# Chain outputs and the second norm's factors: turning on VectorE in 32 by 32 blocks, placed through DRAM

## The chip, the cores and the metric

The kernel runs on one core of a Trainium2 chip. The metric is the device time of one execution in microseconds (us). The profile comes from the hardware profiler and covers one execution. Its engines are PE (TensorE matmuls), PEld (TensorE weight loads, which overlap PE), DVE (VectorE), ACT (ScalarE), POOL (GpSimd) and SP (SyncE). SPq is the queue from which SP issues transfers. On each engine and on SPq, instructions run in the order in which the program placed them.

## What is computed

One layer of a hybrid decoder on 1024 tokens of width 1024, all in float32:

```
h = rmsnorm(x) * norm1_w ; proj = h @ w_in                 # columns split over two mixers
A: gated delta rule, 4 heads of 128, chunked, sequential in the chunks -> o_a
   o_a = rmsnorm(o_a, gdn_norm_w) * silu(z)
B: attention, 8 heads of 64, three dilated windows -> o_b
x = x + concat(o_a, o_b) @ w_out
h = rmsnorm(x, norm2_w)
u = causal_dwconv(h @ w_up) ; x = x + (silu(gate) * up) @ w_down
out = rmsnorm(x, final_norm_w)
```

`gdn_norm_w`, called the output weight here, has one value for each of the 128 columns of a head.

## The kernel before, in words

Most activations lie feature-major: 128 features on the partitions, 1024 tokens along the free dimension. Large products are split into a high and a low part and done in three passes (`mm3`, L200) on 128x512 blocks. Only the chain of the delta rule works with tokens on the partitions.

**Order of the work.** The kernel writes the order of TensorE's instructions by hand. `Weave` (L49) keeps a modelled clock. Work is written as generators ("streams"), each with a level, and the weave always takes the ready stream with the lowest level. A stream yields how long it wants to wait, from modelled ready times of its tiles (`wv.need`). Wrappers for the engines (L152 to L158) add the modelled duration of each instruction and transfer to those times. TensorE's instructions carry a token (`mm` L192, `tp` L196), so they keep the order in which the weave gave them. The instructions of the other engines and of SPq are ordered afterwards by a scheduler with its own timeline, which may move them before instructions that were written earlier. `uv` and `ua` are VectorE and ScalarE with a higher priority there.

**The streams that matter.**

- `dense()` (L532, level 9) runs the input projection column by column: 48 `mm3` passes each, with the next column's weights split one column ahead and the one after that loaded (`take`, L550). It fills whatever the other streams leave free on TensorE. Its last four columns are the gates z of the four chain heads. Column z of head h is taken only when `("o", h)` is done (L585). It then loads `og`, the head's normalised output, from DRAM and multiplies it with silu(z) (L608 to L611).
- `chain(h)` (L844, level 1), one for each head, walks 8 chunks. Each step goes over TensorE, VectorE (`r`, `wke`, the state `sn`) and ScalarE (`w`, `vtok`). At its end GpSimd scales the whole output `vtok` by the norm (L910) and `finish` is added.
- `finish(h, osb)` (L913, level 1) turns the output from token-major to feature-major. For each half of 512 tokens it transposes four 128x128 blocks on TensorE against the identity (`tp`), ScalarE copies the PSUM bank to `ot` with the output weight as its scale (`gw2`, half of `gdn_norm_w`), and one transfer writes 128 rows of 512 floats to `mixer` in DRAM. `ot` takes one of two slots (tag `t2`).
- `attention()` (L946, level 5) waits for `("o", h)` of all four heads and for two dense columns, then for each pair of heads runs scores, softmax, turning and values.
- `out_proj()` (L1144, level 8) takes the mixers' outputs, split in `mixer_splits` (L1119).
- `mlp_up()` (L1379, level 8) does the up projection in 22 channel tiles of 7 half-size products each (P1 to P7, `up`, L1316). `pa` is one PSUM bank in which P1, P6, P7 and P4 add up one after another; ScalarE copies its state after P1, P6 and P7 (`p1`, `u2`, `u3`).

**The second norm.** Each token's factor 1/rms must stand on all 128 partitions, because tokens lie along the free dimension (`rstdB`, 128x1024). In the first channel tile alone (`before is None`), `rms2_power` (L1236) sums the squares over the partitions on TensorE, VectorE adds the epsilon, and GpSimd takes the power -1/2; the result `rs` has 128 tokens on the partitions and 8 columns. P7 follows. Then `rms2_spread` (L1245) transposes each column, broadcast to 128 columns, on TensorE (8 transposes into two banks), and VectorE copies the banks to `rstdB`. P4 follows. VectorE first uses `rstdB` at L1357.

Of the kernel before, what the change touches and what calls it, by code (L numbers as in the profile page):

```python
# [147 lines left out]
def hybrid_layer(tc, I, out):  # L148
# [47 lines left out]
    def tp(dst, src, idt=None, us=0.11):  # L196
        tc.stamp_issue_order_token(nc.tensor.transpose(dst, src, ident if idt is None else idt).ins, TOKEN)  # L197
        wv.product(us, dst, src)
# [50 lines left out]
    def rsqrt(dst, src, n):  # L249
        po_.tensor_tensor(dst, src, mhalf[:, :n], op=OP.pow)  # L250
# [8 lines left out]
    vpark = dp.tile([S, 512], F32, name="vpark")  # L259
    qpark = dp.tile([H, P, S], F32, name="qpark")  # L260
    atpark = dp.tile([H, P, S], F32, name="atpark")
    xpark = dp.tile([KT, P, S], F32, name="xpark")
    upark = dp.tile([FT, P, S], F32, name="upark")

    def bank(tag, name="ps"):
        return tile_(pp_, (P, 512), F32, name, tag, 2)

    def next_bank(tag, *tiles, slack=0.0):

        while max(wv.need(*tiles), wv.slot_free(tag, 2)) + slack > 1e-3:  # L270
            yield max(wv.need(*tiles), wv.slot_free(tag, 2)) + slack
        return bank(tag)

    def half(i):
        return slice(i * 512, i * 512 + 512)
# [236 lines left out]
    def silu2(xr, name):  # L512
        y = A(name, "ev")
        ac.activation(y, xr, AF.Tanh, scale=0.5)
        ve.scalar_tensor_tensor(y, y, 1.0, xr, op0=OP.add, op1=OP.mult)
        return y
# [15 lines left out]
    def dense():  # L532

        yield from wv.until("first")
        yield from wv.until("norms")
        wv.add(2, first_keys())

        srcs, tiles = [], 0
        for col in DENSE:
            if col[0] == "V":  # L540
                srcs += [I["wv"][j] for j in range(4)]
            else:
                srcs.append(I["wi"][tiles])
                tiles += 1
        place = [0]
        raw = [raw_weight(srcs[0])]
        nxt = [weight(None, st=raw.pop())]
        raw.append(raw_weight(srcs[1]))

        def take():  # L550
            w = nxt.pop()
            i = place[0] = place[0] + 1
            if i < len(srcs):
                nxt.append(weight(None, st=raw.pop(), spare=i >= 17))
            if i + 1 < len(srcs):
                raw.append(raw_weight(srcs[i + 1]))
            return w

        def values_by_token(g):

            banks = [bank(t) for t in ("asc", "asc", "ch", "ch")]
            for j in range(4):
                w = [t.rearrange("p (k m) -> p k m", k=2) for t in take()]
                for kk in range(2):
                    k = 2 * j + kk
                    for i, pt in enumerate(banks):
                        c = 4 * g + i
                        yield wv.need(pt, *w)
                        mm3(pt, [t[:, c * P:(c + 1) * P] for t in xs[k]], [t[:, kk, :] for t in w], k == 0, k == KT - 1)
            for i in range(0, 4, 2):  # L570
                vx = A("vx", "ev", shape=(P, 2, 512))
                for e in range(2):
                    c = 4 * g + i + e
                    ac.activation(vx[:, e, :], banks[i + e], AF.Copy, scale=rst[:, c:c + 1])
                c = 4 * g + i
                sy.dma_start(vpark[c * P:(c + 2) * P].rearrange("(e p) d -> p e d", e=2), vx)
            wv.done.add(("V", g))

        for i, col in enumerate(DENSE):
            kind, h = col[:2]  # L580
            if kind == "V":
                yield from values_by_token(h)
                continue
            if kind == "z":
                yield from wv.until(("o", h))  # L585
            w = [t.rearrange("p (k m) -> p k m", k=KT) for t in take()]
            pair = []
            for hh in range(2):
                pt = bank("hf")
                yield wv.need(pt, *w)  # L590
                for k in range(KT):
                    mm3(pt, [t[:, k, :] for t in w], [t[:, half(hh)] for t in xs[k]], k == 0, k == KT - 1)
                    yield 0.0

                pair.append(pt)
                if hh == 0:
                    xr = A("aqkv" if kind == "a" else "xr", "go" if kind == "k" else "ev")
                scaled(pair, "xr", kind == "a", t=xr, hs=(hh,))
            if kind == "k":
                T["k", h] = conv_silu(xr, 4 + h, "kT", "kT*")  # L600
                wv.add(3, kprep(h))
            elif kind == "q":
                q = conv_silu(xr, h, "qT", "qa")
                wv.add(4, qprep(h, q))
            elif kind == "v":
                v = conv_silu(xr, 8 + h, "vT", "qa")
                wv.add(4, vprep(h, v))
            elif kind == "z":  # L608
                og = gated[h] = A("og", "kT*")
                sy.dma_start(og, mixer[h])  # L610
                ve.tensor_tensor(og, og, silu2(xr, "zz"), op=OP.mult)  # L611
            else:
                sy.dma_start(apark[h, col[2]], xr)
                wv.done.add(col)
        wv.done.add("dense")
# [295 lines left out]
        wv.add(1, finish(h, vtok))  # L911

    def finish(h, osb):  # L913
        for hh in range(2):
            pt = yield from next_bank("atr", osb)
            for c in range(4):
                i = 4 * hh + c
                tp(pt[:, c * P:(c + 1) * P], osb[:, i * P:(i + 1) * P])
            ot = tile_(sp, [P, 512], F32, "ot", "t2", 2)
            ac.activation(ot, pt, AF.Copy, scale=gw2)  # L920
            sy.dma_start(mixer[h][:, half(hh)], ot)
        wv.done.add(("o", h))


# [311 lines left out]
    def rms2_power():  # L1236
        ps = bank("atr")
        for c in range(NCH):
            mm(ps[:, c:c + 1], rstdB[:, c * P:(c + 1) * P], ones[:, :1], 0.215)
        rs = sp.tile([P, NCH], F32, name="rs")  # L1240
        uv.tensor_scalar(rs, ps[:, :NCH], 1.0 / 1024, EPS, op0=OP.mult, op1=OP.add)
        rsqrt(rs, rs, NCH)
        return rs

    def rms2_spread(rs):  # L1245
        for h in range(2):
            pb = bank("atr")
            for c in range(4):
                tp(pb[:, c * P:(c + 1) * P], rs[:, 4 * h + c:4 * h + c + 1].to_broadcast([P, P]))
            ve.tensor_copy(rstdB[:, half(h)], pb)  # L1250

    W = {}
    raws = {}
# [62 lines left out]
    def up(n, before):  # L1316

        xg, xu = A("xg", "kT"), A("xu", "kT")
        pa = bank("asc", "pa")
        yield from up_product(n, "P1", pa, True, False)  # L1320
        p1 = tile_(sp, [P, 512], F32, "p1", "t2", 2)
        ac.activation(p1, pa, AF.Copy)
        if before is not None:
            yield from before()
        pc = bank("ch", "pc")
        if before is None:

            yield from up_product(n, "P5", pc, True, False)
            pd = bank("hf", "pd")
            yield from up_product(n, "P2", pd, ks=range(3))  # L1330
        yield from up_product(n, "P6", pa, False, False)
        u2 = tile_(wp, [P, 512], F32, "u2", "wlo", 2)
        last["u2"] = ac.activation(u2, pa, AF.Copy)
        if before is None:
            yield from up_product(n, "P2", pd, False, ks=(3,))
            rs = rms2_power()
        else:
            yield from up_product(n, "P5", pc, True, False)
        yield from up_product(n, "P7", pa, False, False)
        if before is None:  # L1340
            rms2_spread(rs)
        else:
            pd = yield from next_bank("hf")
            yield from up_product(n, "P2", pd)
        u3 = tile_(sp, [P, 512], F32, "u3", "t2", 2)
        last["u3"] = ac.activation(u3, pa, AF.Copy)
        ve.tensor_tensor(xu[:, half(1)], u3, pc, op=OP.add)
        ve.tensor_tensor(xg[:, half(0)], p1, pd, op=OP.add)
        yield from up_product(n, "P4", pa, False, True)
        ac.activation(xu[:, half(0)], pa, AF.Copy)  # L1350

        def rest():
            yield from up_product(n, "P3", pc, False)
            ve.tensor_tensor(xg[:, half(1)], u2, pc, op=OP.add)
            del W[n]
            up_tail(n, xg, xu)
        ve.tensor_tensor(xu, xu, rstdB, op=OP.mult)  # L1357
        last["rest"] = rest
# [332 lines left out]
```

## Time and profile before

| what | before |
|---|---|
| time, median of 3 runs | 1200.84 us (1200.32 to 1201.92) |
| time of the profiled execution | 1200.36 us |
| its span | 1198.6 us |
| mean granted TensorE clock | 0.997 |
| DMA engines over the span | 154.80 MB, mean 129 GB/s |
| TensorE instructions, transposes of `finish` / of the second norm | 7050, of which 32 / 8 |
| chain of the delta rule | ends near 312 us |
| attention on TensorE | 319.5 to 442.8 us |
| second norm's factors | near 567 to 573 us |
| up projection, steady part | 577 to 976 us |

The profiled execution took 1200.36 us, 1.76 us more than its span from first to last instruction. In the views below, times are us from the start of the span unless marked ns. A row of a grouped view gives the line, the engine, the operation, its output and inputs by the program's names, how many there were, the busy time, the mean duration in ns of one, and the idle time of the engine just before them with what ended it. Where a helper issues the instruction, the line is the helper's: L142 and L144 are the engine wrappers, L193 is `mm` and L197 is `tp`. A matmul's row lasts longer than the matmul occupies TensorE, since they are pipelined: the distance from start to start is its cost.

### The profile page before, as it was taken

The numbers are of one execution on the slowest core, as the hardware profiler recorded it, in microseconds if no ns is written. First come the engines' busy times: TensorE is split into PE (matmuls) and PEld (weight loads), VectorE is DVE, ScalarE is ACT, GpSimd is POOL, SyncE is SP. The second block draws the span as 40 slices with busy tenths as digits, with TensorE's granted clock in tenths as the row PEclk, the third lists the DMA queues.
The fourth block names the chain that finished last, engine by engine and source line by source line (L and its number), as shares of the span: only waits on it lengthen the run. The fifth ranks groups of instructions, "written<-read, shape, count | busy, mean of one in ns | idle before, by whom it ended". The sixth has DMA issues, their size and how long they took to land.

```text
span 1198.6 us, 18324 instructions
## 1 busy us (share of the span) xinstructions
PE 1187.5 (99%) x7050; PEld 983.7 (82%) x7050; DVE 915.1 (76%) x1450; ACT 574.8 (48%) x1126; POOL 89.8 (7%) x100
## 2 busy tenths in 40 slices
PE   9999999999999999999999999999999999999997
PEld 7888888888777778888888888888888888888886
DVE  7683975665355566777989888989898889999875
ACT  7275345355454443655544544445445454434441
POOL 0212010214311120000000000000000000000000
PEclk9999999999999999999999999999999999999998
DMA  7435234436634204543213223131222398557414
GB/s 237 107 95 150 85 109 127 152 113 183 224 95 124 73 28 128 180 154 110 88 54 104 90 70 106 53 106 60 99 90 69 109 371 292 192 157 229 160 53 141
DMA packets 85798, 154.80 MB, mean 129 GB/s; under 512 B 21168, under 2 KB 36304, under 8 KB 85712
## 3 DMA queue, kind: packets, MB, share of 16 engines
q1 hardware_dynamic: 84848, 152.85, 39.1%
q8 instruction: 55, 0.90, 0.3%
q10 hardware_dynamic: 864, 0.79, 0.2%
q14 instruction: 31, 0.25, 0.1%
HBM read 117.68 MB, written 35.93 MB: 128 GB/s over the span
## 4 chain that ended last, share of the span: by engine, by line
PE 95%; DVE 2%; ACT 2%; issue 1%; DMA 0%; POOL 0%; POOLq 0%; DVEq 0%; SPq 0%; ACTq 0%
PE ps L193 45%; PE pa L193 20%; PE dw L193 17%; PE pc L193 10%; PE ps L197 3%; DVE kT L142 1%; ACT sm L144 0%; DMA xt<-in_xT 0%; DVE x1h L142 0%; ACT whi L142 0%; PE pd L193 0%; DVE zz L142 0%; ACT dec L142 0%; DVE xr L142 0%; DVE rstdB L142 0%
## 5 line engine op out<-in xcount | busy, mean ns | idle before, releaser
L193 PE MATMUL dw<-pr 128*128 128x512 f32 (+1 forms) x984 | 211.3, 376 | 0.0
L193 PEld LDWEIGHTS dw<-pr 128*128 128x128 f32 x984 | 176.7, 188 | 33.6
L193 PE MATMUL ps<-xhi,whi 128*128 128x512 f32 x384 | 157.7, 411 | 0.3 <-ACT xhi L144 0.3
L193 PE MATMUL ps<-xhi,wlo 128*128 128x512 f32 x384 | 150.3, 391 | 0.0
L193 PE MATMUL ps<-xlo,whi 128*128 128x512 f32 x384 | 148.4, 390 | 0.0
L193 PE MATMUL pa<-T,pair 128*128 128x512 f32 x528 | 127.0, 389 | 0.0
L193 PEld LDWEIGHTS pa<-T,pair 128*128 128x128 f32 x528 | 99.0, 188 | 20.6
L193 PEld LDWEIGHTS ps<-xhi,whi 128*128 128x128 f32 x384 | 72.5, 189 | 19.6 <-issue 5.6
L193 PEld LDWEIGHTS ps<-xhi,wlo 128*128 128x128 f32 x384 | 72.4, 188 | 15.7
L193 PEld LDWEIGHTS ps<-xlo,whi 128*128 128x128 f32 x384 | 72.3, 188 | 12.5
L142 ACT ACTIVATE u<-pa 128x512 f32<-128x512 f32 x44 | 26.3, 598 | 107.2 <-PE pa L193 107.2
L142 DVE SCALAR_TENSOR_TENSOR y<-xu,fcw,y 128x1023 f32<-128x1023 f32 (+1 forms) x44 | 56.4, 1281 | 22.1 <-ACT y L142 22.0
L142 ACT ACTIVATE whi<-wst 128x1024 fp32r<-128x1024 f32 x36 | 38.2, 1063 | 65.4 <-PE ps L193 54.3
L193 PE MATMUL pa<-B,A 128*128 128x512 f32 x264 | 63.4, 389 | 0.0
L193 PE MATMUL pa<-T,S 128*128 128x512 f32 x264 | 63.4, 389 | 0.0
L193 PE MATMUL pc<-B,pair 128*128 128x512 f32 x264 | 63.4, 389 | 0.0
L193 PE MATMUL pc<-T,S 128*128 128x512 f32 x264 | 63.4, 389 | 0.0
L142 DVE TENSOR_TENSOR wst<-wst 128x512 f32<-128x512 f32 x88 | 60.5, 688 | 0.9
L193 PE MATMUL ps<-B,pair 128*128 128x512 f32 x252 | 60.5, 389 | 0.0
L142 POOL TENSOR_TENSOR rs<-rs,mhalf 128x2 f32<-128x2 f32 (+2 forms) x4 | 4.7, 1187 | 738.4 <-DVE rs L144 738.4
L142 ACT ACTIVATE pr<-wd 128x1024 fp32r<-128x1024 f32 x33 | 34.9, 1058 | 49.5 <-PE dw L193 37.0
L144 ACT ACTIVATE sm<-sm,mx 128x128 f32<-128x128 f32 (+7 forms) x64 | 35.4, 556 | 48.2 <-DVE mx L144 48.2
(248 smaller groups left out, 2411.1 us busy)
## 6 DMA issues: line engine op xcount, KB each, us to landing
wst<-in_wu SPq DMA_DIRECT2D x44, 512.0 KB, 3.7
wd<-in_wd SPq DMA_DIRECT2D x44, 512.0 KB, 4.5
upark<-y SPq DMA_DIRECT2D x22, 512.0 KB, 3.6
wst<-in_wi SPq DMA_DIRECT2D x21, 512.0 KB, 3.8
r<-upark SPq DMA_DIRECT2D x11, 512.0 KB, 7.5
r<-upark SPq DMA_DIRECT2D x22, 256.0 KB, 7.5
wa<-in_wd SPq DMA_DIRECT2D x22, 256.0 KB, 3.3
wst<-in_wv SPq DMA_DIRECT2D x8, 512.0 KB, 3.7
```

The lines of the kernel that those rows point to most:

```text
L142: return getattr(eng, op)(*a, **kw)
L144: return getattr(eng, op)(*a, **kw)
L193: tc.stamp_issue_order_token(nc.tensor.matmul(dst, lhs, rhs, start=start, stop=stop, **kw).ins, TOKEN)
L197: tc.stamp_issue_order_token(nc.tensor.transpose(dst, src, ident if idt is None else idt).ins, TOKEN)
```

## The change

1. `finish` no longer uses TensorE or PSUM. VectorE turns each 128x512 half of `osb` in blocks of 32 by 32, which puts the elements of every block in place within it but leaves the blocks where they were. Four transfers per half, one for each group of 32 partitions, then write the pieces to a new DRAM tensor `odram`, in runs of 32 floats.
2. At the gate, four transfers (32 partitions each) in place of one load `og` from `odram`, in runs of 128 floats.
3. The output weight is no longer the scale of ScalarE's copy, which is gone. It joins the multiplication with the gate: one `scalar_tensor_tensor` in place of a `tensor_tensor`.
4. `rms2_spread` is gone. `rs` grows to 128x32, is filled with ones, its first 8 columns get the factors as before, and VectorE turns it by 32 by 32 blocks into `dt`. Four transfers write 8 rows of 32 floats each to `ndram` (1024 floats), and a fifth reads all 1024 floats to each of the 128 partitions of `rstdB`.

```diff
+    ndram = dp.tile([S], F32, name="ndram")
+    odram = dp.tile([H, 32, 4 * S], F32, name="odram")
...
                 og = gated[h] = A("og", "kT*")
-                sy.dma_start(og, mixer[h])
-                ve.tensor_tensor(og, og, silu2(xr, "zz"), op=OP.mult)
+                of = odram[h].rearrange("j (c a t) -> a j c t", c=NCH, a=4)
+                for a in range(4):
+                    sy.dma_start(v8(og)[32 * a:32 * a + 32], of[a])
+                ve.scalar_tensor_tensor(og, og, gw2, silu2(xr, "zz"), op0=OP.mult, op1=OP.mult)
...
     def finish(h, osb):
+        yield wv.need(osb)
         for hh in range(2):
-            pt = yield from next_bank("atr", osb)
-            for c in range(4):
-                i = 4 * hh + c
-                tp(pt[:, c * P:(c + 1) * P], osb[:, i * P:(i + 1) * P])
             ot = tile_(sp, [P, 512], F32, "ot", "t2", 2)
-            ac.activation(ot, pt, AF.Copy, scale=gw2)
-            sy.dma_start(mixer[h][:, half(hh)], ot)
+            ve.transpose(ot, osb[:, half(hh)])
+            to = odram[h].rearrange("j (f b i) -> b j f i", f=32, b=4)[:, :, 16 * hh:16 * hh + 16]
+            for b in range(4):
+                sy.dma_start(to[b], ot[32 * b:32 * b + 32].rearrange("p (f i) -> p f i", i=32))
...
-        rs = sp.tile([P, NCH], F32, name="rs")
-        uv.tensor_scalar(rs, ps[:, :NCH], 1.0 / 1024, EPS, op0=OP.mult, op1=OP.add)
-        rsqrt(rs, rs, NCH)
-        return rs
-
-    def rms2_spread(rs):
-        for h in range(2):
-            pb = bank("atr")
-            for c in range(4):
-                tp(pb[:, c * P:(c + 1) * P], rs[:, 4 * h + c:4 * h + c + 1].to_broadcast([P, P]))
-            ve.tensor_copy(rstdB[:, half(h)], pb)
+        rs = tile_(sp, [P, 32], F32, "rs", "dt", 2)
+        ve.memset(rs, 1.0)
+        uv.tensor_scalar(rs[:, :NCH], ps[:, :NCH], 1.0 / 1024, EPS, op0=OP.mult, op1=OP.add)
+        rsqrt(rs[:, :NCH], rs[:, :NCH], NCH)
+        dt = tile_(sp, [P, 32], F32, "dt", "dt", 2)
+        uv.transpose(dt, rs)
+        to = ndram.rearrange("(c t) -> c t", c=NCH)
+        for b in range(4):
+            sy.dma_start(to[:, 32 * b:32 * b + 32], dt[32 * b:32 * b + NCH, :])
+        sy.dma_start(rstdB, bass.AP(tensor=ndram.tensor, offset=ndram.offset, ap=[[0, P]] + list(ndram.ap)))
...
             yield from up_product(n, "P2", pd, False, ks=(3,))
-            rs = rms2_power()
+            rms2_power()
         else:
             yield from up_product(n, "P5", pc, True, False)
         yield from up_product(n, "P7", pa, False, False)
-        if before is None:
-            rms2_spread(rs)
-        else:
+        if before is not None:
             pd = yield from next_bank("hf")
             yield from up_product(n, "P2", pd)
```

## The prediction

> **What bounds the kernel now.** I read the page first: busy shares, then the chain that ended last.
>
> ```profile
> PE 1187.5 (99%) x7050; PEld 983.7 (82%) x7050; DVE 915.1 (76%) x1450; ACT 574.8 (48%) x1126; POOL 89.8 (7%) x100
> ...
> PE 95%; DVE 2%; ACT 2%; issue 1%; DMA 0%; POOL 0%; POOLq 0%; DVEq 0%; SPq 0%; ACTq 0%
> ```
>
> TensorE is 99% busy and is 95% of the chain: whatever leaves its queue leaves the end time, unless something it waits for becomes late. Busy shares overstate a pipelined engine, so the price of a transpose has to come from the chain in order of time, where each piece is what it adds to the path. These are the pieces on line L197 (`tp`) around the ends of the four chains, and the one of the second norm.
>
> ```profile
> 284.75 0.87 PE ps L197 x8
> ...
> 288.10 0.12 issue
> 288.23 0.63 PE ps L197 x4
> ...
> 290.00 0.44 PE ps L197 x4
> ...
> 299.13 0.44 PE ps L197 x4
> ...
> 300.48 0.44 PE ps L197 x4
> ...
> 311.21 0.87 PE ps L197 x8
> ...
> 570.05 0.87 PE ps L197 x8
> ```
>
> Columns: start, us on the chain, what. All 32 transposes of `finish` stand on the chain, about 0.11 us each, as do the 8 of the norm. Which stages can refill what goes? The table by stages answers that (length, then busy us and instruction count of PE, PEld, DVE, ACT, POOL, then the granted clock, DMA share and GB/s).
>
> ```profile
> 283.00:292.00 9.00, 8.88 (x63) 7.98 (x62) 4.44 (x13) 5.77 (x17) 4.41 (x5) 1.00 0.59 167
> 284.00:320.00 36.00, 35.88 (x203) 30.52 (x203) 11.30 (x26) 14.66 (x37) 15.64 (x10) 1.00 0.72 232
> 320.00:440.00 120.00, 119.61 (x1530) 92.81 (x1527) 70.96 (x243) 60.80 (x205) 23.55 (x45) 1.00 0.29 93
> 440.00:467.00 27.00, 27.00 (x158) 22.41 (x157) 14.70 (x14) 7.83 (x9) 2.40 (x1) 1.00 0.20 57
> ```
>
> From 284 to 320 dense columns fill TensorE between the chain's steps, and at 440 to 467 some 24 us of dense work are still left over after attention. So dense work can move up into every hole that a removed transpose leaves.
>
> **The change part by part.**
>
> *Transposes of `finish`, removed.* The six pieces: 0.87 + 0.63 + 3 x 0.44 + 0.87 = 3.69 us. The 0.12 us of issue ahead of the second may go too or stay; I leave it. **Gain 3.7 us**, bounds 3.3 (the eight sets counted from start to start, with the slower first product behind them kept) and 3.8.
>
> *Transposes of the norm, removed.* What comes next there decides.
>
> ```profile
> 567.08 2.97 PE L193 MATMUL pa<-T,pair 128*128 128x512 f32 x12
> ...
> 567.62 2.06 POOL L142 TENSOR_TENSOR rs<-rs,mhalf 128x8 f32<-128x8 f32 x1 [119.13 <-DVE rs L144]
> ...
> 569.89 1.03 PE L197 MATMUL ps<-ident,rs 128*128 128x128 f32 x8
> 570.15 0.60 ACT L142 ACTIVATE u<-pa 128x512 f32<-128x512 f32 x1 [1.29 <-PE pa L193]
> ...
> 570.80 3.01 PE L193 MATMUL pa<-T,pair 128*128 128x512 f32 x12
> ...
> 575.26 1.22 DVE L142 TENSOR_TENSOR xu<-xu,rstdB 128x1024 f32<-128x1024 f32 x1
> ...
> 579.09 2.88 PE L193 MATMUL pa<-T,S 128*128 128x512 f32 x12
> ```
>
> P7 (567.08) and P4 (570.80) add into the same bank `pa`, and ScalarE must copy its state between them (`u3`, 570.15 to 570.75, released by P7's last product). In later channel tiles P2 covers that copy; in this one P2 was done earlier, and the 8 transposes are the only cover. Take them out and P4 still starts at about 570.80, behind the copy. The 0.87 us turns into idle time. **Gain 0.05 us**, the distance from the copy's end to P4's start; bounds 0 and 0.1.
>
> *VectorE's transposes, added.* The trace has none. Nearest rows:
>
> ```profile
> L142 DVE TENSOR_TENSOR wst<-wst 128x512 f32<-128x512 f32 x88 | 60.5, 688 | 0.9
> ...
> L142 DVE TENSOR_TENSOR aqkv<-ps,rstdB 128x512 f32<-128x512 f32 x16 | 17.8, 1112 | 21.7 <-PE ps L193 21.7
> ```
>
> A plain pass over 128x512 takes 0.69 us, one with scattered columns 1.11. I take 0.69 (both sides are read and written once) and keep 0 and 1.11. Eight make 5.5 us, bounds 0 and 8.9, against 24.7 us in which VectorE is idle between 284 and 320: room in sum. ScalarE loses its eight copies. What is queued behind a transpose on VectorE are the steps `r`, `wke` and the state of the heads still running, and TensorE waits for those in a fixed order. That matters for heads 0 and 1 (283 to 292), where VectorE is busy 4.44 of 9 us; heads 2 and 3 end in quiet stretches. **Loss 0.5 us**: four transposes there, each with an even chance to stand ahead of a due step, half of one (0.34) in the mean, gives 0.7, of which dense products cover a part; bounds 0 and 4 x 0.69 = 2.8. The Trainium skill (VectorE: DVE Perf Modes, The three transpose paths) gives 311 ns for a 128x128 bf16 turn on VectorE and advises TensorE for 128x128. By an estimate from that page a half would take 1.24 us and the loss would be 0.9. No run so far shows it.
>
> *Transfers, added.* SPq issues 32 writes and 16 loads in place of 8 and 4, and 5 for the norm.
>
> ```profile
> L142 SPq DMA_DIRECT2D x<-xdram x8: 319/484/487, 173.6 to 181.1; - x8
> ...
> q1 hardware_dynamic: 8203, 1.01, 48.8%
> ...
> q1 hardware_dynamic: 975, 0.15, 52.7%
> ...
> L142 DVE TENSOR_TENSOR og<-og,zz x4: 1224/1225/1226, 424.4 to 470.3; 128x1024 f32<-128x1024 f32 x4
> ...
> 301.30 0.39 SPq L142 DMA_DIRECT2D wst<-in_wi  x1
> ...
> wst<-in_wi SPq DMA_DIRECT2D x2, 512.0 KB, 4.5
> ...
> 322.27 1.04 ACT L142 ACTIVATE whi<-wst 128x1024 fp32r<-128x1024 f32 x1
> ```
>
> The first row is a transfer of 512 pieces of 128 bytes, as each new write is: 0.484 us to issue. So 36 more issues cost SPq some 17 us over 40 us. The two queue rows price a piece: in 173 to 186 us (reads of 128 bytes) 0.488 x 13 x 16 / 8203 = 12.4 ns; in 111.5 to 113.7 us (writes of 128 bytes) 0.527 x 2.2 x 16 / 975 = 19 ns. The new writes are 32 x 512 pieces: 16384 x 19 / 16 = 19.5 us of all engines. The old writes, 2.1 MB at 232 / 0.72 = 322 GB/s, took 6.5. The stretch of 36 us, 25.8 us full, then needs about 39: the queue falls some 3 us behind, and the loads of `og` in short rows may double that. What is late then? `og` is loaded soon after 290 and used at 424.4 at the earliest, as its row shows. The tightest transfer behind it is a weight tile: issued at 301.30, landing 4.5 us later, split at 322.27, so 16 us spare. **Cost 0**, and 1 us for each us beyond 16 if that cover goes.
>
> *Gate.* Four `scalar_tensor_tensor` stand for four `tensor_tensor` of the same size, one pass each, beside dense products from 424 us on. **0**, bounds 0 and the 0.4 us by which the scattered pass above exceeds the plain one, if the last head's gate were to end a wait.
>
> *The factors through DRAM.* The power ends at 569.68, the turn of 128x32 about 0.2 later; SPq is free there.
>
> ```profile
> wst<-in_wu SPq DMA_DIRECT2D x44, 512.0 KB, 3.7
> ...
> dec<-gdram SPq DMA_DIRECT2D x4, 512.0 KB, 7.6
> ...
> gdram<-grow SPq DMA_DIRECT2D x1, 16.0 KB, 1.4
> ...
> 577.73 0.33 SPq L142 DMA_DIRECT2D wst<-in_wu  x1
> ```
>
> Four issues (1.6), a small write landing (1.4 to 2.0) and a 512 KB read: 3.7 as a weight tile, 7.6 as the other broadcast, which had three more beside it. I take 3.7: `rstdB` at about 577.3, bounds 576.5 and 581.5, against 575.26 where VectorE used it. VectorE is held about 2 us (bounds 0 and 6); behind it stand the weight splits of the next channel tile, and on SPq the weight load of 577.73. The first product needing one of the held splits comes 5 us or more later (the next `pa<-T,S` at 579.09 has its operand by 573.6), so it stays hidden; **cost 0**, bounds 0 and 1.
>
> *Order.* The weave models every added transfer at 0.78 us on SPq (per-half writes) and 1.5 (loads), so attention, which starts 8 us after the last `finish`, is placed about 4 us later, with dense columns in front of it. TensorE idles 0.39 us in attention's 120, so a new order can't win there; **0** taken, loss up to the third rival's price.
>
> **Sum** against the profiled span: 1198.6 - 3.7 - 0.05 + 0.5 = 1195.35; with the 1.76 us around it 1197.1. The median of the runs, 1200.84, lies 0.48 above the profiled execution's 1200.36, so against the median I say **1197.5**.
>
> **The rivals.**
>
> *Half of the gain more* (1195.5): the slower first products and the issue gaps go as well, and the handover costs nothing. Price: the gain at its upper bound of 3.8 with the loss of 0.5 gone is 1196.6, and a dense product behind each of eight sets, slowed today by the switch, may give another 1.1. For: the pieces of 0.44 and 0.87 hold only the transposes. Against: chain steps of the same kind stand next to most sets and keep that cost.
>
> *No change: `ot`'s two slots hold VectorE* (1200.4).
>
> ```profile
> mixer<-ot SPq DMA_DIRECT2D x8, 256.0 KB, 4.4
> ...
> 285.43 1.90 POOL L142 TENSOR_TENSOR vtok<-vtok,ms 128x1024 f32<-128x1024 f32 x1
> ...
> 289.02 0.69 ACT L142 ACTIVATE ot<-ps,gw 128x512 f32<-128x512 f32 x1 [0.23 <-DMA mixer<-ot]
> ...
> 291.84 0.35 DVE L144 TENSOR_SCALAR wke<-ps,ke 128x128 f32<-128x128 f32 x1 [2.37 <-PE ps L193]
> ```
>
> Head 1 ends 4 us after head 0 and needs the same two slots, each free only when four small transfers have landed. Head 0's first half, issued from 284.5, lands near 289, its second near 291.5; head 1's output is ready at 287.3. If both turns sit in VectorE's queue at that time, it is held 1.7 + 1.8 = 3.5 us with chain steps behind, which eats the 3.7. For: the old transfers took 4.4 us to land here, and 0.23 us of such a wait stands in the trace of ScalarE. Against: VectorE idles 2.37 us at 289.5 anyway, and the scheduler puts a turn where it believes the slot free.
>
> *Slower: attention in its new order waits for the softmax* (1204.6).
>
> ```profile
> PEld ps L197 <- ACT sm L144: 2.5, 12, 0.4
> ```
>
> Today 12 of attention's 32 turns wait for ScalarE's exponentials, 2.5 us in all, 0.4 the longest. The order is made so that dense products lie in between; shifted by 4 us and with columns pulled ahead, the gaps fall elsewhere. If all 32 wait 0.4 us, that is 12.8, or 10.3 more: 1207; with the mean of 0.21 it is 6.7, or 4.2 more: 1201.4; I price it between at 7.4 more. It decides from 6.1 us (3.7 and the 2.4 that count as slower). For: the weave's slacks suit one order. Against: 24 us of dense work remain to fill with.
>
> *Slower: short writes are dear* (1216). If a written piece of 128 bytes costs over 30 ns, the stretch to 320 needs 25.8 - 6.5 + 1024 x 0.030 = 50 us, 14 behind, and the weight tile comes late; at four times the read piece, 50 ns, it is 34 behind and TensorE waits some 19 us. Against: the measured 19 ns. The Trainium skill (DMA: Bandwidth & Descriptors, Specifications) says that transfers under 512 bytes are done as read-modify-write, which is this case; the 19 against 12.4 ns agree in direction only.
>
> **How the numbers follow.** 0.2% is 2.4 us, about what a measurement of this kernel tells from no change: faster means below 1198.4, slower above 1203.2. Chances: forecast 0.46, the larger gain 0.06, `ot`'s slots 0.23, softmax 0.18, short writes 0.07. Hence faster 0.52, same 0.23, slower 0.25. The forecast's own range is 1196.3 to 1198.4. To hold 8 in 10, the range takes the larger gain's lower side at 1195.0 and the middle of the softmax rival at 1204.5; the rest of that one and the short writes, under 2 in 10, stay out.
>
> **What would show it.** Right: no L197 piece between 284 and 312; P4 of the first channel tile still behind ScalarE's copy with a hole of 0.8 us on TensorE; the multiplication by `rstdB` released by a transfer 1 to 3 us later than now, and TensorE gapless behind it; `og` landed tens of us before use. Wrong: VectorE's transposes with an idle time ended by `odram` transfers and chain products waiting; attention's turns with more than 2.5 us behind ScalarE; a weight split waiting for its transfer; or TensorE idle over 1 us between 575 and 600.

## The result, and the profile after

| | before | after |
|---|---|---|
| time, median of 4 runs | 1200.64 us (1200.32 to 1201.92, taken beside those of after) | 1215.85 us (1214.26 to 1217.01) |
| ratio to before | 1 | 1.0127, 95% interval [1.0114, 1.014] |
| span of the profiled execution | 1198.6 us | 1212.5 us |
| mean granted TensorE clock | 0.997 | 0.992 |

The kernel became 15 us slower. The forecast was 1197.5, and the range ended at 1204.5. The busy shares on the page of after:

```profile
PE 1190.8 (98%) x7010; PEld 983.7 (81%) x7010; DVE 914.8 (75%) x1458; ACT 569.3 (47%) x1118; POOL 90.1 (7%) x100
```

TensorE has 40 instructions fewer and is busy 3.3 us longer, and its idle time in the span grew from 11.1 to 21.7 us. So something both holds it and slows it down. The table by stages of after says where (columns as in the prediction):

```profile
284.00:320.00 36.00, 34.34 (x175) 28.63 (x173) 16.16 (x34) 9.63 (x30) 15.18 (x11) 1.00 0.85 196
...
440.00:460.00 20.00, 14.63 (x208) 11.28 (x209) 17.60 (x45) 15.12 (x42) 1.87 (x7) 0.92 0.47 147
460.00:470.00 10.00, 8.13 (x98) 5.49 (x96) 5.89 (x18) 5.68 (x18) 0.59 (x2) 0.67 0.15 51
470.00:484.00 14.00, 13.06 (x139) 9.41 (x136) 5.65 (x18) 5.08 (x16) 0.59 (x2) 0.86 0.12 39
```

Between 440 and 484 TensorE idles 5.37 + 1.87 + 0.94 = 8.2 us, and the granted clock falls to 0.92, 0.67 and 0.86. A low clock costs only while TensorE works, so its price is taken from steps of 2 us: busy time times the missing share of the clock is 6.0 us (the rows and the sum stand in the last section). Together that is 14.2 us. In the kernel before, the same stretch was full at clock 1.00. What TensorE waited for there stands in the waits of after between 320 and 490 (waiter, releaser, us in total, times, longest) and in its timeline:

```profile
PEld ps L197 <- ACT sm L144: 11.6, 22, 3.0
...
PE ps L197 <- ACT sm L144: 7.4, 12, 2.8
```

```profile
455.56 0.92 PE L197 MATMUL ps<-ident,sm 64*128 64x64 f32 x12 [2.77 <-ACT sm L144]
457.62 0.58 PE L197 MATMUL ps<-ident,sm 64*128 64x64 f32 x6 [1.14 <-ACT sm L144]
```

Attention's turns wait for the exponentials, as in the prediction's third rival, but here TensorE has nothing at all to do in between. The reason is older than 440. The starts of attention's groups of scores on TensorE, first in before and then in after:

```profile
319.54 0.93 PE L193 MATMUL ps<-kT,qT 64*128 64x128 f32 x8
324.07 1.47 PE L193 MATMUL ps<-kT,qT 64*128 64x256 f32 x40
330.33 1.68 PE L193 MATMUL ps<-kT,qT 64*128 64x256 f32 x40
```

```profile
325.53 0.93 PE L193 MATMUL ps<-kT,qT 64*128 64x128 f32 x8
336.88 1.47 PE L193 MATMUL ps<-kT,qT 64*128 64x256 f32 x40
364.91 1.68 PE L193 MATMUL ps<-kT,qT 64*128 64x256 f32 x40
```

The third group comes 34.6 us later than before, and in the gap TensorE is full: it does dense columns. The gate of the last dense columns shows how far these ran ahead: it ran from 424.4 to 470.3 before, and runs from 375.0 to 452.6 now.

```profile
L142 DVE SCALAR_TENSOR_TENSOR og<-og,gw,zz x4: 1252/1254/1268, 375.0 to 452.6; 128x1024 f32<-128x1024 f32 x4
```

The dense work that used to lie between attention's steps until 467 is used up early, and the last part of attention stands alone.

### The profile page after: what moved, and what is told of

The parts are those of the page before. It is cut to its first block, busy times and chain, and to the rows that moved or that the text cites. A ratio compares the mean times of both kernels' runs of the same rounds, so it can differ in the third digit from the quotient of the medians.

```text
span 1212.5 us, 18290 instructions
## 1 busy us (share of the span) xinstructions
PE 1190.8 (98%) x7010; PEld 983.7 (81%) x7010; DVE 914.8 (75%) x1458; ACT 569.3 (47%) x1118; POOL 90.1 (7%) x100
## 4 chain that ended last, share of the span: by engine, by line
PE 91%; ACT 3%; DVE 3%; issue 1%; DMA 1%; SPq 0%; POOLq 0%; POOL 0%; DVEq 0%; ACTq 0%
PE ps L193 43%; PE pa L193 20%; PE dw L193 17%; PE pc L193 10%; PE ps L197 2%; ACT sm L144 1%; DVE kT L142 1%; DMA ot<-mixer 1%; DMA xt<-in_xT 0%; ACT whi L142 0%; DVE x1h L142 0%; ACT zz L142 0%; PE pd L193 0%; DVE og L142 0%; DVE oT L142 0%
## 5 line engine op out<-in xcount | busy, mean ns | idle before, releaser
L142 ACT ACTIVATE pr<-r 128x1024 fp32r<-128x1024 f32 (+1 forms) x44 | 36.5, 839 | 49.2 <-PE dw L193 29.0
```

What stands on the lines that cost most here:

```text
L142: return getattr(eng, op)(*a, **kw)
```

## The experiments

**Theory.** The order is made by the weave's clock, and the clock is wrong about the new writes. `account`, the function that enters an instruction or a transfer into that clock, lets an entry begin only when every tensor that it names is ready. All writes name `odram`, so each is charged behind the landing of the one ahead: 0.78 + 2.2 = 2.98 us apiece. The turn of head 3's second half needs the `ot` slot that was filled two halves earlier, and so the 24th write, 24 x 2.98 = 71.5 us after the first. Until then the clock keeps that head's `vtok`, whose slot (tag `dv*`) attention's softmax takes next. Counted from the first write's issue at 283.5 that is 355, on a clock that runs some us apart from the trace; the trace has the third group at 364.91. This way through `ot` and `vtok` is read from the program; no run isolates it. On the chip, the writes do not wait for each other: head 0's eight were issued in 4.14 us, where the clock charges 8 x 2.98 = 23.8, and a write landed in 2.0 us (median). These are after's rows of the queue and of the transfers:

```profile
283.46 4.14 SPq L142 DMA_DIRECT2D odram<-ot  x8
```

```profile
odram<-ot SPq DMA_DIRECT2D x32, 64.0 KB, 2.0
```

**Rivals:** the short transfers are themselves slow (the prediction's last rival, which named 1216), or VectorE's turns and `ot`'s slots hold the chain.

The times of this section are medians of up to 11 runs, each with its ratio to before on the same chip. Before was 1200.21 beside e1 to e4, 1200.26 beside e5 to e8 and 1199.84 beside e9 to e12. The ratio can differ from that of the two medians by up to 0.06%, or 0.7 us.

### e1_model: after, with the clock charged as in before

```diff
-                    sy.dma_start(v8(og)[32 * a:32 * a + 32], of[a])
+                    nc.sync.dma_start(v8(og)[32 * a:32 * a + 32], of[a])
+                wv.account("sync", 0.05 + 0.00142 * 1024, [og], [odram], 2.2)
...
-                sy.dma_start(to[b], ot[32 * b:32 * b + 32].rearrange("p (f i) -> p f i", i=32))
+                nc.sync.dma_start(to[b], ot[32 * b:32 * b + 32].rearrange("p (f i) -> p f i", i=32))
+            wv.account("sync", 0.05 + 0.00142 * 512, [odram], [ot], 2.2)
```

> The changed kernel with every instruction and transfer kept; only the weave's clock is charged as before: one transfer of 0.78 us per half and one of 1.50 us for og, in place of four each, which the clock puts one behind the other because all four write the same tensor. Theory A (the loss is an order of products made for transfers that the clock took to be long: attention's third group of scores placed 28 us late, dense columns used up ahead of it): attention's groups come every 7 us from the first on, dense products last past attention, 1197.5 us, between 1196 and 1199.5. Theory B (the loss is on the chip: short writes and a held queue): 1211 or more, as the same transfers run. Theory C (both, VectorE held by ot's two slots near 287 us): 1199.5 to 1202.

Measured: **1198.63 us, ratio 0.9991 [0.9982, 1.0000]**. The same instructions and the same transfers as after, 17.2 us less (16.3 by the two ratios). Its rows for the stretch of above, and its third group of scores:

```profile
440.00:460.00 20.00, 20.00 (x89) 16.55 (x89) 11.25 (x10) 5.08 (x6) 2.40 (x1) 1.00 0.18 52
460.00:470.00 10.00, 9.88 (x43) 7.52 (x42) 8.18 (x8) 4.98 (x6) 0.00 (x0) 1.00 0.58 174
470.00:484.00 14.00, 14.00 (x64) 11.58 (x63) 6.03 (x9) 4.84 (x8) 0.00 (x0) 1.00 0.35 122
```

```profile
331.22 1.68 PE L193 MATMUL ps<-kT,qT 64*128 64x256 f32 x40
```

The hole and the low clock are gone; the third group of scores starts at 331.22. The profiled span is 1196.6 us, 15.9 less than that of after, and the 14.2 us found above are most of it; the other 1.7 us are not assigned. This refutes the short writes as the cause: the number that rival gave was right by accident.

### e2_clock: before, with the clock charged as in after

```diff
+                for _ in range(3):
+                    wv.account("sync", 0.05 + 0.00142 * 1024, [og], [mixer], 2.2)
                 sy.dma_start(og, mixer[h])
...
+            wv.account("vector", 0.0, [ot], [osb], 0.28)
             sy.dma_start(mixer[h][:, half(hh)], ot)
+            for _ in range(3):
+                wv.account("sync", 0.05 + 0.00142 * 512, [mixer], [ot], 2.2)
```

> The kernel before, with no instruction or transfer added; only its clock is charged with the entries of the changed kernel (three more transfers per half in finish, three more for og, and a turn on VectorE that needs ot's slot). Theory A: the order alone costs it, attention ends after the dense products and stands without cover: 1212 to 1220 us. Theory B: nothing on the chip changed, 1200.6, at most 2 us more.

Measured: **1221.58 us, ratio 1.0184 [1.0169, 1.0200]**. No instruction of the change is in it, and it loses 21.4 us, more than after did; its time lies 1.6 us above the expected range. Its clock is not that of after in every entry: the tensor that its entries share is `mixer`, to which attention's outputs go as well. Its tail has the same picture, first the wait, then a row of its table by stages:

```profile
PEld ps L197 <- ACT sm L144: 15.4, 22, 7.1
```

```profile
460.00:480.00 20.00, 9.66 (x134) 6.53 (x118) 12.13 (x30) 9.55 (x24) 0.59 (x2) 0.64 0.38 125
```

### e9_single: after, with every transfer charged by itself

This is what the prediction took the clock to do. `Own` is a name that no other entry shares.

```diff
+                    wv.account("sync", 0.05 + 0.00142 * 1024, [og if a == 3 else Own(("og", h, a))], [Own((h, 1, 3))], 2.2)
...
+                wv.account("sync", 0.05 + 0.00142 * 512, [Own((h, hh, b))], [ot], 2.2)
```

> This is the whole change with every one of its transfers charged in the modelled clock by itself (0.78 us of SPq for each write, 1.5 for each load, no transfer waiting for another one's tensor), which is what the prediction assumed of the clock. If the slow order comes from the writes being charged one behind another through the one DRAM tensor, the clock now releases the chain's tiles 1.5 to 3.5 us after each finish instead of 20 to 45, attention gets back the order of before, and the time is that of e1_model: 1198.6 (1198.0 to 1199.3). If the mere number of charged transfers on SPq is what spoils the order, the time stays above 1203 and attention's turns wait for the exponentials 5 us or more.

Measured: **1199.08 us, ratio 0.9996 [0.9987, 1.0004]**. Attention begins late, at 325.70, as in after, but the third group follows at 336.64, and the turns' wait is small (the class `Own` moves the lines of this kernel by six, so L199 is `mm`, L203 is `tp` and L150 the wrapper):

```profile
336.64 1.68 PE L199 MATMUL ps<-kT,qT 64*128 64x256 f32 x40
```

```profile
PEld ps L203 <- ACT sm L150: 1.8, 9, 0.4
```

So the number of charged transfers does no harm that the time shows, and a late start of attention does none either. What does it is that they are charged one behind another. This run frees the loads of `og` as well as the writes, so the share of each is not told apart.

### e3_norm: before, with the norm part alone

```diff
-            rs = rms2_power()
+            rms2_power()
...
-        if before is None:
-            rms2_spread(rs)
-        else:
+        if before is not None:
```

(with `rms2_power` as in the change)

> The kernel before with the second norm's part of the change alone (turn of 128x32 on VectorE, four small writes, one broadcast read). By the prediction's step: P4 still starts behind ScalarE's copy, so 0.05 us gained and nothing lost, 1200.6 us, between 1199.9 and 1201.2, with a hole of 0.8 us on TensorE ahead of P4. Rival: VectorE held some 3 us by the read delays weight splits and TensorE waits, 1202 or more.

Measured: **1200.34 us, ratio 1.0002 [0.9993, 1.0011]**. The norm part is worth nothing that the time shows. After's rows for TensorE (the product that sums the squares, P7, P4) say why:

```profile
579.26 1.84 PE L193 MATMUL ps<-ones,rstdB 128*128 128x1 f32 x16
580.96 2.97 PE L193 MATMUL pa<-T,pair 128*128 128x512 f32 x12
584.68 3.01 PE L193 MATMUL pa<-T,pair 128*128 128x512 f32 x12 [0.75 <-ACT u L142]
```

P4 waits for ScalarE's copy. From the start of the sum of squares to P7's it is 1.70 us here and was 1.70 before; to P4's it is 5.42 and was 5.42. Eight transposes went, and a hole of about their length came.

### e4_chain: the chain part alone, with the clock of e1_model

The norm is that of before; the rest is e1_model.

> The clock charged as in e1_model, the chain's part of the change kept, the second norm as before. Theory A with the norm's part worth nothing: as e1_model within 0.5 us, 1197.5. If the norm's part costs anything on the chip, this one is faster than e1_model by that much (1 us or more if VectorE's wait for the read reaches TensorE).

Measured: **1198.54 us, ratio 0.9988 [0.9979, 0.9997]**. The chain part nets 1.7 us (1.4 by the ratio) where its 32 transposes were priced at 3.7. The next runs ask where the other 2 us are. In the stretch from 284 to 320 TensorE idles 1.56 us, where before idled 0.12. After has the same two holes, shown by its TensorE rows and by VectorE's. `r,um` is the product whose result `wke` scales:

```profile
282.87 0.38 PE L193 MATMUL ps<-r,um 128*128 128x128 f32 x2
285.77 0.49 PE L193 MATMUL ps<-wke,ktok 128*128 128x128 f32 x2 [0.91 <-ACT w L144]
290.23 0.49 PE L193 MATMUL ps<-ct,kT 128*128 128x128 f32 x2 [0.75 <-DVE ct L144]
```

```profile
282.72 0.71 DVE L142 STREAM_TRANSPOSE ot<-vtok 128x512 f32<-128x512 f32 x1
283.58 0.70 DVE L142 STREAM_TRANSPOSE ot<-vtok 128x512 f32<-128x512 f32 x1
284.20 1.03 DVE L142 TENSOR_TENSOR aqkv<-ps,rstdB 128x512 f32<-128x512 f32 x1
285.10 0.32 DVE L144 TENSOR_SCALAR wke<-ps,ke 128x128 f32<-128x128 f32 x1
287.02 0.71 DVE L142 STREAM_TRANSPOSE ot<-vtok 128x512 f32<-128x512 f32 x1 [0.37 <-DMA odram<-ot]
289.24 0.71 DVE L142 STREAM_TRANSPOSE ot<-vtok 128x512 f32<-128x512 f32 x1 [0.76 <-DMA odram<-ot]
```

Head 0's turns and a dense `aqkv` stand ahead of `wke`, and ScalarE's `w` follows `wke`: 0.91 us. Head 1's turns wait for `ot`'s slots (0.37 and 0.76), with chain steps behind: 0.75 us. In e4_chain the two holes are 0.92 and 0.65. The second is the prediction's "no change" rival, in its place and smaller.

### e5_unplaced and e6_slots: fewer transfers, and other slots

The edits against e4_chain, first that of e5_unplaced (its gate loads in one transfer too; it leaves out the placing of the blocks), then that of e6_slots:

```diff
-            for b in range(4):
-                nc.sync.dma_start(to[b], ot[32 * b:32 * b + 32].rearrange("p (f i) -> p f i", i=32))
+            sy.dma_start(mixer[h][:, half(hh)], ot)
```

```diff
-            ot = tile_(sp, [P, 512], F32, "ot", "t2", 2)
+            ot = G[h]["kT"][:, half(hh)]
```

> This is e4_chain with the placing of the blocks left out: each half goes to the mixer tensor as one 256 KB transfer in rows of 512 floats, and the gate loads its output in one transfer, so the 32 by 32 blocks of the chain's output stay where VectorE left them (this part of the computation is left out). Modelled clock and VectorE's turns are those of e4_chain. If the many short transfers cost something by themselves (ot's slots free late, head 1's turns waiting 0.44 and 0.66 us), the time falls: the waits of VectorE's turns for a transfer go below 0.3 us each, TensorE's wait of 0.65 us at ct goes, and the kernel takes 1197.5 to 1198.1. If the waits stem from two slots being too few whatever the transfers' shape, the waits stay and the time stays within 0.3 us of e4_chain's 1198.5. The short-write rival of the prediction would ask for several us less.

> This is e4_chain with each turned half written into the head's own k tile, which is dead by then, in place of the two shared slots. If the slots are what holds VectorE at head 1 (the prediction's second rival), both waits of the turns for a landing (0.44 and 0.66 us) and TensorE's 0.65 us at ct go: 1197.6 to 1198.0. If the turns hurt by their own 0.71 us in VectorE's queue, ahead of chain steps, the waits for landings go but TensorE's waits of 0.6 to 0.9 us on w and ct stay, and the time stays at 1198.3 to 1198.7.

Measured: e5_unplaced **1198.58, ratio 0.9990 [0.9982, 0.9999]**; e6_slots **1198.19, ratio 0.9982 [0.9973, 0.9991]**. In both, the turns no longer wait for a landing and the wait at `ct` is gone; the wait for `w` stays at 0.9 in both, and TensorE idles 0.99 us from 284 to 320. Each theory was half right: the slots are the smaller hole, and closing it changed the time by 0.4 us at most (0.7 by the ratios), which the runs can't tell from nothing. The many short transfers by themselves cost nothing that the time shows (1198.58 without them, 1198.54 with them).

### e7_late and e10_after_chain: turns out of the chain's way

e7_late holds the turns of heads 0 and 1 back in the weave. The scheduler still put head 0's where they were, so e10_after_chain also gives them tiles that become free late.

```diff
+        if h < 2:
+            yield from wv.until(("c", h + 2, NCH - 1))
```

```diff
-            ot = tile_(sp, [P, 512], F32, "ot", "t2", 2)
+            ot = G[h + 2][("kT", "ktok")[hh]][:, half(1)] if h < 2 else tile_(sp, [P, 512], F32, "ot", "t2", 2)
```

> This is e4_chain with the turns of heads 0 and 1 held back until the last chunk of heads 2 and 3 is under way. If all that the chain part lost on the way from 3.7 to 1.7 us lies in the turns standing ahead of chain steps on VectorE (TensorE's waits of 0.92 for w and 0.65 for ct), the waits go and the time falls by about 1.5 us to 1196.9 (1196.5 to 1197.4). If what was removed from TensorE simply comes back as idle time elsewhere in the chain (its steps are bound by their own sequence), the time stays at 1198.2 to 1198.8.

> This is e7_late with the turned halves of heads 0 and 1 put into the dead halves of k tiles of heads 2 and 3, so that VectorE cannot turn them until the chain of those heads has all but passed; the order of TensorE stays. If head 0's turns hold wke on VectorE (my reading of e4_chain's wait of 0.92 us for w), that wait of TensorE goes. If the wait is the chain's own, of wke behind the dense column's aqkv of 1.04 us, and the 8 transposes had merely covered it in the kernel before, then it stays at 0.8 to 0.95 us although no turn stands ahead of it. The time can tell the two apart only weakly: 1197.0 against 1197.8.

Measured: e7_late **1197.84, ratio 0.9981 [0.9972, 0.9990]**, a miss: 0.9 us above what was expected, because only head 1's turns moved and the 0.9 for `w` stayed. e10_after_chain **1196.72, ratio 0.9974 [0.9965, 0.9984]**. Its TensorE, its VectorE and its stretch:

```profile
283.71 0.38 PE L193 MATMUL ps<-r,um 128*128 128x128 f32 x2
285.55 0.47 PE L193 MATMUL ps<-wke,ktok 128*128 128x128 f32 x2
```

```profile
283.91 1.10 DVE L142 TENSOR_TENSOR aqkv<-ps,rstdB 128x512 f32<-128x512 f32 x1
284.85 0.31 DVE L144 TENSOR_SCALAR wke<-ps,ke 128x128 f32<-128x128 f32 x1
286.32 0.71 DVE L142 STREAM_TRANSPOSE ktok<-vtok 128x512 f32<-128x512 f32 x1
```

```profile
284.00:320.00 36.00, 35.70 (x182) 29.87 (x182) 17.25 (x35) 10.56 (x30) 16.64 (x11) 1.00 0.76 178
```

`aqkv` still stands ahead of `wke`, the turns now stand behind, and TensorE's product with `wke` waits for nothing. From `r,um` to `wke` it is 2.23 us in after and 1.14 here, and to TensorE's product with `wke` 2.90 and 1.84. So it was the two turns of 0.7 us, not the dense step. The other reading in the expectation, that the transposes had only filled a wait of the chain's own, falls.

### e11_cover0: head 0's transposes kept beside VectorE's turns

```diff
+            if h == 0:
+                pt = yield from next_bank("atr", osb)
+                for c in range(4):
+                    i = 4 * hh + c
+                    tp(pt[:, c * P:(c + 1) * P], osb[:, i * P:(i + 1) * P])
```

> This is e4_chain with the 8 transposes of head 0 kept on TensorE in their old place, their result unused. If they stood in a wait of the chain anyway, TensorE's wait of 0.92 us for w falls below 0.2 and the time stays within 0.3 us of e4_chain's 1198.5. If they cost what the prediction took for them, 0.87 us, the wait stays and the time is 1199.4.

Measured: **1198.88, ratio 0.9992 [0.9983, 1.0001]**, with the wait for `w` at 0.72 instead of 0.92. The time lies between the two expectations, and its interval covers both: it decides nothing. The trace says more: from `r,um` to the product with `wke` it is 2.89 us, as in e4_chain (2.90), though the 8 transposes now stand there in place of a set of three dense products. What TensorE does meanwhile does not set that distance.

### e8_cover and e12_best: what the two parts can be worth

e8_cover is e1_model with e7_late's hold and the last piece of P2 moved between P7 and P4. e12_best adds e10_after_chain's tiles and 0.9 us of slack ahead of head 2's last product with `wke`.

```diff
-            yield from up_product(n, "P2", pd, False, ks=(3,))
             rms2_power()
...
         if before is not None:
...
+        else:
+            yield from up_product(n, "P2", pd, False, ks=(3,))
```

```diff
-                yield wv.need(wke, slack=HOP)
+                yield wv.need(wke, slack=HOP + (0.9 if h == 2 and c == 6 else 0.0))
```

> This is e1_model (the whole change, with the clock charged as before) with the late turns of e7_late, and with the last piece of P2 in the first channel tile moved between P7 and P4, where the 8 transposes had covered ScalarE's copy of pa. If the norm part is worth nothing only because that copy stands uncovered, TensorE's wait of 0.7 us for u goes and the 0.87 us of the 8 transposes counts: 0.7 to 0.9 us below e7_late, about 1196.1. If instead the factors' way through DRAM holds the multiplication by rstdB, or P2's last piece was itself cover for the power of the norm, a wait of TensorE of 0.5 us or more appears elsewhere between 565 and 580 and the time is that of e7_late within 0.3 us.

> This is e8_cover with the late turns of e10_after_chain, and with one more dense pass placed ahead of head 2's last product with wke (its slack in the modelled clock is 0.9 us longer), to cover the wait for w. If the two waits left in the chain (0.9 for w, 0.3 for ct) are a matter of order alone, both go and the stretch from 284 to 320 has TensorE idle for less than 0.4 us: 1196.7 (1196.0 to 1197.4). If the chain's latency is what bounds that stretch, the idle time turns up at another step of the chain and the time stays at 1197.6 to 1198.2.

Measured: e8_cover **1197.92, ratio 0.9982 [0.9973, 0.9991]**; e12_best **1195.84, ratio 0.9965 [0.9953, 0.9978]**. e8_cover's trace shows the step, its time does not: the cover lies in the hole, and from the sum of squares to P4 it is 5.43 us with 0.68 us more work in it (the piece of P2, second row).

```profile
561.75 1.84 PE L193 MATMUL ps<-ones,rstdB 128*128 128x1 f32 x16
566.27 0.84 PE L193 MATMUL pd<-B,pair 128*128 128x512 f32 x3
567.18 3.01 PE L193 MATMUL pa<-T,pair 128*128 128x512 f32 x12
```

The median is level with e7_late's, and the runs of each spread over 2.5 to 4 us, so 0.7 us can't be told there. e12_best has no idle TensorE from 284 to 320 and is faster than both kernels:

```profile
284.00:320.00 36.00, 36.00 (x186) 29.59 (x185) 17.30 (x42) 10.96 (x31) 16.91 (x11) 1.00 0.79 171
```

## Why the prediction was wrong, step by step

**The step that failed is "Order".** It said that the weave "models every added transfer at 0.78 us on SPq" and so shifts attention by about 4 us, at a cost of 0. e9_single is that assumption as a kernel, and there it holds: attention starts 6 us later and the time shows no loss. The clock of after does something else. The prediction read the entry's duration and not its start, which waits for the tensor that all the writes share. Where it looked at slots, it looked at the tile that is written, `ot`, and not at the tile that is read, `vtok`, whose slot attention needs. Price of the step: 1215.85 - 1198.63 = 17.2 us (16.3 by the ratios), against 0 taken. Without it the kernel stands at 1198.63, 1.1 us above the forecast; the items on VectorE's turns and `ot`'s slots are of that size.

**The softmax rival** had the right wait and the wrong price, 1204.6 with bounds 1201.4 and 1207. It took 0.4 us at most for each turn, from a row in which dense work covered the rest, and "24 us of dense work remain to fill with" spoke against it. That dense work was what the new order used up first. Without it the turns waited up to 2.8 us, and the clock that fell behind the holes added 6.0 us, a term the prediction did not have.

**Transposes of `finish`, 3.7 us:** the sum behind this holds. TensorE's busy time fell from 1187.5 us to 1183.6 in e4_chain, which removes these 32 alone, and once the holes are closed, e12_best stands 1199.84 - 1195.84 = 4.0 us below before (interval 2.6 to 5.6), with the 0.7 us of e8_cover's step in it if that counts.

**VectorE's turns, loss 0.5 with bounds 0 and 2.8:** the duration was right (0.706 median against 0.69). The loss was mis-sized: of e4_chain's 1.56 us of idle TensorE from 284 to 320, 0.92 are behind head 0's turns. The even chance of standing ahead of a due step was too kind: both turns of head 0 did. **`ot`'s slots**, priced at the whole 3.7, took the other 0.65 (0.75 in after).

**The norm:** gain 0.05 said, ratio 1.0002 measured, with the hole of 0.75 us that was foretold as 0.8. The factors' read landed 4.4 us after its issue (3.7 taken), VectorE waited 3.1 us for it (2 taken, at most 6), and TensorE lost nothing behind it. **The gate:** 1.25 us for one pass against 1.22, hidden. **Transfers:** 504 ns to issue a write against 484, and cost 0 as said. The stretch from 284 to 320 took 0.82 x 36 = 29.5 us of the DMA engines in e4_chain, where the prediction counted 39, though some of the last writes fall behind 320; `og` was issued from 294.2 to 326.7 and first used at 375.0.

What stays open: 1.7 us of e4_chain's gain and the 3.7 removed differ by 2.0, of which 1.56 - 0.12 = 1.4 is shown as idle time; the rest is within the spread of the runs.

## What to carry to other kernels

Where a hand-made planner orders the work, put the change through the planner's arithmetic before pricing the chip: which shared name does each new entry wait for, and which tile's release hangs on its end. Charge several transfers that fill parts of one tensor as one entry, or under names of their own. And work that fills gaps is a stock: ask of a new order not only whether there is enough of it, but whether it is still left when the last gaps come.

## What the runs showed of the hardware

**A hole costs TensorE twice.** The table of after in steps of 2 us:

```profile
452.00:454.00 2.00, 0.78 (x36) 0.44 (x34) 2.00 (x3) 0.07 (x1) 0.00 (x0) 1.00 0.74 261
454.00:456.00 2.00, 0.40 (x6) 0.27 (x6) 2.00 (x9) 2.00 (x5) 0.00 (x0) 1.00 0.82 242
456.00:458.00 2.00, 0.79 (x12) 0.65 (x12) 1.79 (x5) 1.63 (x6) 0.30 (x1) 0.70 0.85 321
458.00:460.00 2.00, 1.51 (x18) 1.21 (x18) 1.46 (x5) 2.00 (x8) 0.30 (x1) 0.50 0.13 34
460.00:462.00 2.00, 2.00 (x14) 1.50 (x12) 1.12 (x2) 0.98 (x4) 0.00 (x0) 0.50 0.75 255
462.00:464.00 2.00, 2.00 (x38) 0.77 (x36) 1.78 (x5) 0.80 (x2) 0.00 (x0) 0.60 0.00 0
464.00:466.00 2.00, 0.85 (x13) 0.53 (x12) 1.71 (x10) 1.86 (x6) 0.28 (x1) 1.00 0.00 0
466.00:468.00 2.00, 1.28 (x16) 1.03 (x18) 0.93 (x4) 1.73 (x7) 0.31 (x2) 0.76 0.00 0
468.00:470.00 2.00, 2.00 (x24) 1.67 (x22) 0.35 (x2) 0.32 (x2) 0.00 (x0) 0.50 0.00 0
470.00:472.00 2.00, 2.00 (x20) 1.65 (x18) 1.07 (x1) 0.00 (x0) 0.00 (x0) 0.50 0.00 0
472.00:474.00 2.00, 2.00 (x37) 0.73 (x33) 0.42 (x1) 0.00 (x0) 0.00 (x0) 0.54 0.39 139
```

After 4 us with 1.2 us of work the granted clock falls to 0.50 and stays low until 464, although TensorE is full again from 460. A second hole, 2.1 us of work in the 4 us from 464, brings it down again until 474. Busy time times the missing share of the clock, row by row from 456, is 0.24 + 0.76 + 1.00 + 0.80 + 0 + 0.31 + 1.00 + 1.00 + 0.92 = 6.0 us. The Trainium skill (TensorE: Matmul & The Clock Gate, What's actually happening) has two states, full and half, and an idle window of about 3.4 us that leads from one to the other; the 0.50 here agrees. The window itself is not shown: the longest wait in TensorE's rows above was 2.77 us.

**VectorE's turn costs what a plain pass does.** One 128x512 half in float32 took 0.706 us (median of 8), and 128x32 took 0.21. The prediction's estimate from the Trainium skill (VectorE: DVE Perf Modes, The three transpose paths) was 1.24 us for a half; the measurement decides.

**Short writes were cheaper than feared.** In the 36 us from 284, the DMA engines were busy 0.82 of the time in e4_chain and 0.67 in e5_unplaced, which has none of them, so the 36 additional transfers and their short pieces took about 0.15 x 36 = 5.4 us of engine time there. The other kernels with the same transfers and the clock charged as in before lie between 0.76 and 0.87, which makes it 3 to 7 us. In e4_chain TensorE waited for no weight tile in that stretch.
